# Per-token factors spread over the partitions: transposes of a column read with step zero in place of a diagonal and a product of ones

## The chip, the cores and the metric

The kernel runs on one core of one Trainium2 chip. The metric is the device time of one execution in microseconds (us). The kernel before was run three times: median 2529.21 us, from 2528.57 to 2531.68.

## The reference

Two layers of an encoder over 272 tokens (16 learned meta tokens ahead of 256), model width 2048, all in float32. Per layer:

```
h = rmsnorm(x)                                   # per token: x * rsqrt(mean(x*x) + eps) * g
q, k, v, f, ga, gf = split(h @ w_in)             # 8 query heads, 2 key heads of 128
q, k = rope(rmsnorm(q)), rope(rmsnorm(k))        # per head and token
a = attention(q, k, v) @ w_attn_br
s = real(fft2(f over tokens and group channels)) @ w_four
x = x + (sigmoid(ga + b) * a + sigmoid(gf + b) * s) @ w_out
h2 = rmsnorm(x)
x = x + (silu(conv3(h2 @ w_up_gate)) * (h2 @ w_up_val)) @ w_down
```

The meta tokens are dropped at the end. What matters here is the per-token factor of the norms: one number for each of 272 tokens, four times in the run (two norms in each of two layers), and for the keys one number for each token and each of two key heads, in each layer.

## The kernel before

**Layout.** The residual stream `XT` lies transposed: 128 channels on the partitions, 16 channel tiles, the 272 tokens along the free axis. A factor per token must therefore stand in all 128 partitions as a row of 272 numbers, `rstdB`, before the vector engine can multiply by it.

**Weights.** Each matrix comes in chunks of 512 KB (`raw`, L240, issued from SyncE's queue, four or more ahead). ScalarE rounds a chunk to a high part `wh` (L277), VectorE subtracts for the low part `wl` (L279), and TensorE makes three matmuls per tile, high by high, high by low and low by high (L348 to L350, L416 to L418 in the first groups). `wh` and `wl` have three buffers each, so ScalarE can start on a chunk only when TensorE has left the one three back.

**Order of work.** `group` walks through the chunks. After every second tile of a chunk, that is after six matmuls, it calls `step()` (L290), which lets one of the pending side jobs run one piece. The side jobs are generators pushed with `push`: the norm statistics, the key statistics, the Fourier stages, attention and others. The number that a generator yields is the count of steps that it then waits. `until` and `drain` run steps without matmuls between them. So a job's yields decide between which matmuls its own TensorE instructions stand. The tile framework's planner may still shift instructions against each other on an engine where it is not told to keep the order. Each engine serves its own queue in order.

**Norm statistics** (`norm_stats`, L574). The squares of all channel tiles are added up in `acc`. Three transposes (L582; the 16 meta tokens are repeated to 128 columns in `am`, L576) put the tokens on the partitions, VectorE reduces and scales them to `ms` (L584, L585), and GpSimd raises to the power -0.5 (`pow_half`, L489). `tok` then holds the factors as three columns: column 0 the 16 meta tokens (repeated), columns 1 and 2 the two blocks of 128 tokens. Four steps later VectorE multiplies a constant mask, two identity matrices beside a block for the meta tokens, with the columns of `tok`, which gives the diagonals `dg` (L592, three instructions). Two steps after that one float32 product of a matrix of ones and `dg` sums over the partitions (L595), so that each partition of `ps_nb` holds the whole row. ScalarE copies it to `rstdB` (L596).

**Key statistics** (`kstats`, L943). The same for the keys: transposes in `sums_t` (L911), reduction, power (`rk`), and for each of the two heads a diagonal `dk` (L955, three instructions) and, five steps later, a product with the ones (L958). VectorE multiplies the result into the keys `kp` (L959). Then the keys are swapped by four DMAs from SyncE's queue (L917) and rotated (L921 to L926).

The mask sits in the constants `cst`; mask and identity are loaded together (L426) after the first matmuls. `ones` is set by GpSimd at the start (L468).

Of the kernel before, what the change touches and what calls it, by code (L numbers as in the profile page):

```python
# [10 lines left out]
F32 = mybir.dt.float32  # L11
F32R = mybir.dt.float32r
AF = mybir.ActivationFunctionType
ALU = mybir.AluOpType
AX = mybir.AxisListType

P = 128
D = 2048
NM = 16
SEQ = 256  # L20
T = NM + SEQ
# [52 lines left out]
TH = T // 2 + 2  # L74
BLK = ((0, 16), (16, 144), (144, 272))

C_COS, C_SIN, C_MASK = 0, T, 2 * T
C_ID = 3 * T
C_CC = C_ID + P
C_SC = C_CC + HC1  # L80
C_BR = C_SC + HC1
# [13 lines left out]
def _constants():  # L95
    f32 = np.float32
    pairs = HD // 4
    inv = (f32(1.0) / np.power(f32(ROPE_THETA), np.arange(pairs, dtype=f32) / f32(pairs)).astype(f32)).astype(f32)
    tok = np.arange(SEQ)
    zm = np.zeros(NM, f32)  # L100
    pos_r = np.concatenate([zm, (tok // GRID_W).astype(f32)])
    pos_c = np.concatenate([zm, (tok % GRID_W).astype(f32)])
    ar = (pos_r[None, :] * inv[:, None]).astype(f32).astype(np.float64)
    ac = (pos_c[None, :] * inv[:, None]).astype(f32).astype(np.float64)
    cos = np.concatenate([np.cos(ar), np.cos(ar), np.cos(ac), np.cos(ac)], 0)
    sin = np.concatenate([-np.sin(ar), np.sin(ar), -np.sin(ac), np.sin(ac)], 0)
    eye = np.eye(P)
    m16 = (np.arange(P)[:, None] % NM == np.arange(NM)[None, :]) / (P // NM)
    mask = np.concatenate([m16, eye, eye], 1)
    j = np.arange(P)  # L110
    ang = 2.0 * np.pi * ((j[:, None] * j[None, :]) % P) / P
    cc = (np.cos(ang) / math.sqrt(P))[:, :HC1]
    sc = (np.sin(ang) / math.sqrt(P))[:, :HC1]
    sc[:, 0] = sc[:, HC] = 0.0
    n = np.arange(T)
    angl = 2.0 * np.pi * ((n[:, None] * n[None, :]) % T) / T
    cl = np.cos(angl) / math.sqrt(T)
    sl = -np.sin(angl) / math.sqrt(T)
    b0 = cl[0:128, :TH]
    b1 = sl[1:129, :TH]  # L120
    br = np.zeros((NM, 2, TH))
    br[0:9, 0] = cl[128:137, :TH]
    br[9:16, 1] = sl[129:136, :TH]
    br = np.tile(br.reshape(NM, 2 * TH), (NG, 1))
    gm = (np.arange(P)[:, None] // NM == np.arange(NG)[None, :]).astype(np.float64)
    consts = np.concatenate([cos, sin, mask, eye, cc, sc, br, gm], 1).astype(f32)
    bmat = np.concatenate([b0, b1], 1).astype(f32)
    return np.ascontiguousarray(consts), np.ascontiguousarray(bmat)

# [25 lines left out]
def encoder_kernel(ctx, tc, xT, params, consts, bmat, cfold, csign, w_fl, w_f64c, w_in, w_abr, w_four, w_f64, w_out, w_up, w_down, w_vn, w_dn, w_dt, out):  # L155
# [236 lines left out]
    def first_groups(pss):  # L392
# [4 lines left out]
        for kt in range(KT // CW * 2 * CW):  # L397
# [25 lines left out]
                pump(len(chunks))  # L423
            if kt == 0:
                tc.keep_in_program_order(nc.sync.dma_start(XT[:, 12:16, :], xT[:, 12:16, :]))
                tc.keep_in_program_order(nc.sync.dma_start(cst[:, C_MASK:C_CC], consts[:, C_MASK:C_CC]))  # L426
            step()


# [3 lines left out]
    xH, xL = xHL[:, :, 0, :], xHL[:, :, 1, :]  # L433
    prm = per.tile([P, P_N], F32, name="prm")
    cst = per.tile([P, C_N], F32, name="cst")
    ones = per.tile([P, P], F32, name="ones")
    warm = per.tile([P, 1], F32, name="warm")
    mhalf = per.tile([P, 24], F32, name="mhalf")
    BH = per.tile([P, 2, TH], F32R, name="BH")
# [25 lines left out]
    load_raw(3)  # L465
    st["raw"] = 4
    tc.keep_in_program_order(nc.sync.dma_start(XT[:, 8:12, :], xT[:, 8:12, :]))
    nc.gpsimd.memset(ones, 1.0)  # L468
    nc.gpsimd.memset(V3.bitcast(F32), 0.0)
    nc.gpsimd.memset(o64.bitcast(F32), 0.0)  # L470
    nc.gpsimd.memset(o64m, 0.0)
# [2 lines left out]

    cos = cst[:, C_COS:C_COS + T]
    sin = cst[:, C_SIN:C_SIN + T]
    mask = cst[:, C_MASK:C_MASK + T]
    ident = cst[:, C_ID:C_ID + P]
    ccm = cst[:, C_CC:C_CC + HC1]
    scm = cst[:, C_SC:C_SC + HC1]  # L480
# [68 lines left out]
    def weight_sums():  # L549
# [7 lines left out]
        for s_ in range(1, len(VSETS)):  # L557
# [6 lines left out]
            for q, base, more in kinds:  # L564
                for j in range(NV // 2 + 1):
# [3 lines left out]
                    if j:  # L569
                        issue(dst(q, j - 1), more(j - 1), accum_op=ALU.add, max_dma_last_dim=4096)  # L570
                        ready_sums.update((s_, q, 2 * j - 2 + k) for k in range(2))
                        yield 1

    def norm_stats(holder, gap=0):  # L574
        am = small.tile([P, P // NM, NM], F32, tag="am", name="am", bufs=1)
        nc.vector.tensor_copy(am, _rep(acc[:, 0:NM], P // NM))  # L576
# [9 lines left out]
        tok = small.tile([P, 3], F32, tag="tok", name="tok")  # L586
        pow_half(tok, ms)
        holder["tok"] = tok
        yield 4
        dg = small.tile([P, T], F32, tag="sq", name="dg", bufs=2)  # L590
        for i, (a, b) in enumerate(BLK):
            nc.vector.tensor_scalar(dg[:, a:b], mask[:, a:b], tok[:, i:i + 1], None, op0=ALU.mult)  # L592
        yield 2
        pb = psum.tile([P, 512], F32, tag="aux", name="ps_nb")
        nc.tensor.matmul(pb[:, :T], ones, dg, start=True, stop=True)  # L595
        nc.scalar.copy(rstdB, pb[:, :T])  # L596
        tok2 = small.tile([P, 3], F32, tag="tok2", name="tok2")
        nc.vector.tensor_tensor(tok2, tok, tok, op=ALU.mult)
# [5 lines left out]
    for l in range(DEPTH):  # L604
# [6 lines left out]
        with tc.tile_pool(name=f"mix{l}", bufs=1) as mp:  # L611
# [23 lines left out]
            def ut(name):  # L635
                return mp.tile([P, T], F32, tag="u", name=name, bufs=2)
# [80 lines left out]
            if l == 0:  # L717
# [10 lines left out]
                pss = []  # L728
                push(sums(pss), 4)
                first_groups(pss)  # L730
                for dst, src in ((cst[:, 0:C_MASK], consts[:, 0:C_MASK]), (cst[:, C_CC:], consts[:, C_CC:]), (prm[:, P_BG:], params[:, P_BG:])):
                    tc.keep_in_program_order(nc.sync.dma_start(dst, src))
                bt = rt("bt")
                bt = bt[:, :, :TH]
# [208 lines left out]
            def kstats():  # L943
# [4 lines left out]
                nc.vector.tensor_scalar(kss, kss, 1.0 / HD, EPS, op0=ALU.mult, op1=ALU.add)  # L948
                rk = small.tile([P, 2, 3], F32, tag="rk", name="rk")
                pow_half(rk.rearrange("p a b -> p (a b)"), kss.rearrange("p a b -> p (a b)"))  # L950
                yield 6
                for kv in range(NKV):
                    dk = ut("dk")
                    for i, (a, b) in enumerate(BLK):
                        nc.vector.tensor_scalar(dk[:, a:b], mask[:, a:b], rk[:, kv, i:i + 1], None, op0=ALU.mult)  # L955
                    yield 5
                    pk = psum.tile([P, 512], F32, tag="aux", name="ps_kb")
                    nc.tensor.matmul(pk[:, :T], ones, dk, start=True, stop=True)  # L958
                    nc.vector.tensor_tensor(kp[:, kv, :], kp[:, kv, :], pk[:, :T], op=ALU.mult)  # L959
                yield 3  # L960
                qs = swap(kp)
# [602 lines left out]
```

## Time and profile before

| what | value |
|---|---|
| median of three runs | 2529.21 us |
| the profiled execution | 2531.8 us |
| its span, first to last instruction | 2529.8 us |
| instructions in the span | 47935 |
| mean granted TensorE clock | 1.000 |
| mean DMA rate | 279 GB/s |

The profile is of one execution. The span is a little shorter than the time of that execution, since something lies around it. The engines are PE (TensorE's matmuls), PEld (its weight loads, which overlap the matmuls), DVE (VectorE), ACT (ScalarE), POOL (GpSimd) and SP (SyncE, which issues most DMAs). A group of the profile is named by its line, engine, operation and tiles, `out<-in`; `L592` is line 592 of the kernel before. Matmuls are pipelined and their ends are modelled, so the distance from one start to the next tells what one of them costs, and its own duration does not.

### The profile page before, as it was taken

The numbers are of one execution on the slowest core, as the hardware profiler recorded it, in microseconds if no ns is written. First come the engines' busy times: TensorE is split into PE (matmuls) and PEld (weight loads), VectorE is DVE, ScalarE is ACT, GpSimd is POOL, SyncE is SP. The second block draws the span as 40 slices with busy tenths as digits, with TensorE's granted clock in tenths as the row PEclk, the third lists the DMA queues.
The fourth block names the chain that finished last, engine by engine and source line by source line (L and its number), as shares of the span: only waits on it lengthen the run. The fifth ranks groups of instructions, "written<-read, shape, count | busy, mean of one in ns | idle before, by whom it ended". The sixth has DMA issues, their size and how long they took to land.

```text
span 2529.8 us, 47935 instructions
## 1 busy us (share of the span) xinstructions
PE 2517.8 (100%) x18848; PEld 2435.4 (96%) x18848; DVE 1985.4 (78%) x3151; ACT 1343.6 (53%) x1921; POOL 205.2 (8%) x393
## 2 busy tenths in 40 slices
PE   9999999999999999999999999999999999999999
PEld 9999999999999999999999999999988889998887
DVE  7687866778878667888768887666778787898898
ACT  5455434554444334444445555444676665666665
POOL 0000000012212222222200000000000000000000
PEclk9999999999999999999999999999999999999999
DMA  6444557879999999999975647888888887788887
GB/s 238 164 151 161 192 189 248 260 267 374 393 330 373 398 378 378 386 376 390 384 274 184 201 149 237 258 256 260 272 257 292 297 290 239 258 281 290 276 303 269
DMA packets 194771, 706.85 MB, mean 279 GB/s; under 512 B 22113, under 2 KB 27361, under 8 KB 194289
## 3 DMA queue, kind: packets, MB, share of 16 engines
q1 hardware_dynamic: 146768, 517.09, 58.3%
q0 software_dynamic: 46336, 184.57, 21.1%
q8 instruction: 147, 2.41, 0.4%
q10 hardware_dynamic: 1440, 2.13, 0.2%
q14 instruction: 80, 0.65, 0.1%
HBM read 623.32 MB, written 111.15 MB: 290 GB/s over the span
## 4 chain that ended last, share of the span: by engine, by line
PE 97%; DMA 1%; DVE 1%; ACT 0%; issue 0%; SPq 0%; DVEq 0%; ACTq 0%
PE ps_p L1404 14%; PE ps_ug L350 7%; PE ps_ug L349 7%; PE ps_ug L348 7%; PE ps_d L349 4%; PE ps_uv L349 4%; PE ps_d L348 3%; PE ps_uv L350 3%; PE ps_d L350 3%; PE ps_uv L348 3%; PE ps_o L349 2%; PE ps_o L348 2%; PE ps_o L350 2%; PE ps_gf L349 2%; PE ps_gf L348 2%; PE ps_gf L350 2%
## 5 line engine op out<-in xcount | busy, mean ns | idle before, releaser
L279 DVE TENSOR_TENSOR wl<-raw,wh 128x1024 fp32r<-128x1024 f32 (+1 forms) x961 | 1158.4, 1217 | 408.9 <-ACT wh L277 398.8
L277 ACT CAST wh<-raw 128x1024 fp32r<-128x1024 f32 (+1 forms) x961 | 999.7, 1045 | 900.8 <-PE ps_ug L349 217.2
L349 PE MATMUL ps_ug<-xHL,wh 128*128 128x272 f32 (+1 forms) x1408 | 401.5, 285 | 0.0
L348 PE MATMUL ps_ug<-xHL,wh 128*128 128x272 f32 (+1 forms) x1408 | 400.8, 285 | 0.0
L350 PE MATMUL ps_ug<-xHL,wl 128*128 128x272 f32 (+1 forms) x1408 | 400.4, 286 | 0.0
L349 PEld LDWEIGHTS ps_ug<-xHL,wh 128*128 128x128 f32 x1408 | 264.7, 188 | 3.2
L348 PEld LDWEIGHTS ps_ug<-xHL,wh 128*128 128x128 f32 x1408 | 264.6, 188 | 3.3
L350 PEld LDWEIGHTS ps_ug<-xHL,wl 128*128 128x128 f32 x1408 | 264.0, 188 | 1.4 <-DVE wl L279 1.0
L1404 PE MATMUL ps_p<-wh,opnd 128*128 128x512 f32 x816 | 222.8, 393 | 0.0
L349 PE MATMUL ps_uv<-xHL,wh 128*128 128x272 f32 x704 | 203.3, 289 | 0.0
L349 PE MATMUL ps_d<-gHL,wh 128*128 128x272 f32 x704 | 202.9, 288 | 0.0
L348 PE MATMUL ps_d<-gHL,wh 128*128 128x272 f32 x704 | 202.9, 288 | 0.0
L350 PE MATMUL ps_uv<-xHL,wl 128*128 128x272 f32 x704 | 202.6, 288 | 0.0
L348 PE MATMUL ps_uv<-xHL,wh 128*128 128x272 f32 x704 | 202.3, 287 | 0.0
L350 PE MATMUL ps_d<-gHL,wl 128*128 128x272 f32 x704 | 202.1, 287 | 0.0
L1404 PEld LDWEIGHTS ps_p<-wh,opnd 128*128 128x128 f32 x816 | 148.4, 188 | 29.6 <-ACT wh L277 0.2
L348 PE MATMUL ps_ga<-xHL,wh 128*128 128x272 f32 (+1 forms) x512 | 147.8, 289 | 0.0
L348 PE MATMUL ps_gf<-xHL,wh 128*128 128x272 f32 (+1 forms) x512 | 146.8, 287 | 0.4 <-DVE so L1197 0.4
L510 DVE TENSOR_TENSOR wi<-wi,wi 128x512 f32<-128x512 f32 x224 | 146.9, 684 | 0.0
L349 PE MATMUL ps_o<-mL,wh 128*128 128x272 f32 (+1 forms) x512 | 146.5, 286 | 0.0
L349 PE MATMUL ps_ga<-xHL,wh 128*128 128x272 f32 (+1 forms) x512 | 146.1, 285 | 0.0
L350 PE MATMUL ps_o<-mH,wl 128*128 128x272 f32 (+1 forms) x512 | 146.1, 285 | 0.0
(378 smaller groups left out, 5970.2 us busy)
## 6 DMA issues: line engine op xcount, KB each, us to landing
raw<-in_w_up SPq DMA_DIRECT2D x288, 512.0 KB, 6.4
raw<-in_w_in SPq DMA_DIRECT2D x191, 512.0 KB, 3.9
raw<-in_w_down SPq DMA_DIRECT2D x88, 512.0 KB, 6.9
wi<-in_w_dn POOLq DMA_DIRECT2D x80, 512.0 KB, 8.9
ft<-wi POOLq DMA_DIRECT2D x80, 512.0 KB, 7.4
raw<-ft SPq DMA_DIRECT2D x80, 512.0 KB, 4.6
raw<-in_w_out SPq DMA_DIRECT2D x64, 512.0 KB, 4.3
raw<-fv SPq DMA_DIRECT2D x64, 512.0 KB, 4.8
```

What stands on the lines that cost most here:

```text
L277: nc.scalar.copy(h[:, a:b], r[:, a:b])
L279: nc.vector.tensor_tensor(lo[:, a:b], r[:, a:b], h[:, a:b].bitcast(F32), op=ALU.subtract)
L348: nc.tensor.matmul(o, h[:, c, sl], a, start=kt == 0, stop=False)
L349: nc.tensor.matmul(o, h[:, c, sl], b, start=False, stop=False)
L350: nc.tensor.matmul(o, lo[:, c, sl], a, start=False, stop=kt == nk - 1)
L510: tt = lambda *v, **kw: tc.keep_in_program_order(nc.vector.tensor_tensor(*v, **kw))
L1404: nc.tensor.matmul(ps[h], x, w[:, 512 * h:512 * h + 512], start=fresh and (s_, q) in BEGIN and first, stop=(s_, q) in END and end, skip_gr ...
```

## The change

A helper `spread` takes a column of factors and, for each of the three token blocks, makes a transpose on TensorE: the column is read with step zero along the free axis, so that it looks like a block of 128 equal columns; its transpose has the factors along the free axis, the same in all 128 partitions. `spread` takes the place of diagonal and product in `norm_stats` and in `kstats`. The two yields around the diagonal become one: in `norm_stats` 4 and 2 become 5; in `kstats` 6, and 5 for each head, become 7 for both heads together. The meta tokens' block takes 16 partitions and a 16 by 16 identity. The mask leaves the constants (272 columns fewer in `cst` and in the load at L426), and `ones` goes with its memset.

```diff
@@ -74,8 +74,8 @@
 TH = T // 2 + 2
 BLK = ((0, 16), (16, 144), (144, 272))
 
-C_COS, C_SIN, C_MASK = 0, T, 2 * T
-C_ID = 3 * T
+C_COS, C_SIN = 0, T
+C_ID = 2 * T
 C_CC = C_ID + P
 C_SC = C_CC + HC1
 C_BR = C_SC + HC1
@@ -105,8 +105,6 @@
     cos = np.concatenate([np.cos(ar), np.cos(ar), np.cos(ac), np.cos(ac)], 0)
     sin = np.concatenate([-np.sin(ar), np.sin(ar), -np.sin(ac), np.sin(ac)], 0)
     eye = np.eye(P)
-    m16 = (np.arange(P)[:, None] % NM == np.arange(NM)[None, :]) / (P // NM)
-    mask = np.concatenate([m16, eye, eye], 1)
     j = np.arange(P)
     ang = 2.0 * np.pi * ((j[:, None] * j[None, :]) % P) / P
     cc = (np.cos(ang) / math.sqrt(P))[:, :HC1]
@@ -123,7 +121,7 @@
     br[9:16, 1] = sl[129:136, :TH]
     br = np.tile(br.reshape(NM, 2 * TH), (NG, 1))
     gm = (np.arange(P)[:, None] // NM == np.arange(NG)[None, :]).astype(np.float64)
-    consts = np.concatenate([cos, sin, mask, eye, cc, sc, br, gm], 1).astype(f32)
+    consts = np.concatenate([cos, sin, eye, cc, sc, br, gm], 1).astype(f32)
     bmat = np.concatenate([b0, b1], 1).astype(f32)
     return np.ascontiguousarray(consts), np.ascontiguousarray(bmat)
 
@@ -423,7 +421,7 @@
                 pump(len(chunks))
             if kt == 0:
                 tc.keep_in_program_order(nc.sync.dma_start(XT[:, 12:16, :], xT[:, 12:16, :]))
-                tc.keep_in_program_order(nc.sync.dma_start(cst[:, C_MASK:C_CC], consts[:, C_MASK:C_CC]))
+                tc.keep_in_program_order(nc.sync.dma_start(cst[:, C_ID:C_CC], consts[:, C_ID:C_CC]))
             step()
 
 
@@ -433,7 +431,6 @@
     xH, xL = xHL[:, :, 0, :], xHL[:, :, 1, :]
     prm = per.tile([P, P_N], F32, name="prm")
     cst = per.tile([P, C_N], F32, name="cst")
-    ones = per.tile([P, P], F32, name="ones")
     warm = per.tile([P, 1], F32, name="warm")
     mhalf = per.tile([P, 24], F32, name="mhalf")
     BH = per.tile([P, 2, TH], F32R, name="BH")
@@ -465,7 +462,6 @@
     load_raw(3)
     st["raw"] = 4
     tc.keep_in_program_order(nc.sync.dma_start(XT[:, 8:12, :], xT[:, 8:12, :]))
-    nc.gpsimd.memset(ones, 1.0)
     nc.gpsimd.memset(V3.bitcast(F32), 0.0)
     nc.gpsimd.memset(o64.bitcast(F32), 0.0)
     nc.gpsimd.memset(o64m, 0.0)
@@ -474,7 +470,6 @@
 
     cos = cst[:, C_COS:C_COS + T]
     sin = cst[:, C_SIN:C_SIN + T]
-    mask = cst[:, C_MASK:C_MASK + T]
     ident = cst[:, C_ID:C_ID + P]
     ccm = cst[:, C_CC:C_CC + HC1]
     scm = cst[:, C_SC:C_SC + HC1]
@@ -571,6 +566,11 @@
                         ready_sums.update((s_, q, 2 * j - 2 + k) for k in range(2))
                         yield 1
 
+    def spread(ps, cols):
+        for i, (a, b) in enumerate(BLK):
+            n = b - a
+            nc.tensor.transpose(ps[:, a:b], cols[0:n, i:i + 1].to_broadcast([n, P]), ident[0:n, 0:n])
+
     def norm_stats(holder, gap=0):
         am = small.tile([P, P // NM, NM], F32, tag="am", name="am", bufs=1)
         nc.vector.tensor_copy(am, _rep(acc[:, 0:NM], P // NM))
@@ -586,13 +586,9 @@
         tok = small.tile([P, 3], F32, tag="tok", name="tok")
         pow_half(tok, ms)
         holder["tok"] = tok
-        yield 4
-        dg = small.tile([P, T], F32, tag="sq", name="dg", bufs=2)
-        for i, (a, b) in enumerate(BLK):
-            nc.vector.tensor_scalar(dg[:, a:b], mask[:, a:b], tok[:, i:i + 1], None, op0=ALU.mult)
-        yield 2
+        yield 5
         pb = psum.tile([P, 512], F32, tag="aux", name="ps_nb")
-        nc.tensor.matmul(pb[:, :T], ones, dg, start=True, stop=True)
+        spread(pb, tok)
         nc.scalar.copy(rstdB, pb[:, :T])
         tok2 = small.tile([P, 3], F32, tag="tok2", name="tok2")
         nc.vector.tensor_tensor(tok2, tok, tok, op=ALU.mult)
@@ -728,7 +724,7 @@
                 pss = []
                 push(sums(pss), 4)
                 first_groups(pss)
-                for dst, src in ((cst[:, 0:C_MASK], consts[:, 0:C_MASK]), (cst[:, C_CC:], consts[:, C_CC:]), (prm[:, P_BG:], params[:, P_BG:])):
+                for dst, src in ((cst[:, 0:C_ID], consts[:, 0:C_ID]), (cst[:, C_CC:], consts[:, C_CC:]), (prm[:, P_BG:], params[:, P_BG:])):
                     tc.keep_in_program_order(nc.sync.dma_start(dst, src))
                 bt = rt("bt")
                 bt = bt[:, :, :TH]
@@ -948,14 +944,10 @@
                 nc.vector.tensor_scalar(kss, kss, 1.0 / HD, EPS, op0=ALU.mult, op1=ALU.add)
                 rk = small.tile([P, 2, 3], F32, tag="rk", name="rk")
                 pow_half(rk.rearrange("p a b -> p (a b)"), kss.rearrange("p a b -> p (a b)"))
-                yield 6
+                yield 7
                 for kv in range(NKV):
-                    dk = ut("dk")
-                    for i, (a, b) in enumerate(BLK):
-                        nc.vector.tensor_scalar(dk[:, a:b], mask[:, a:b], rk[:, kv, i:i + 1], None, op0=ALU.mult)
-                    yield 5
                     pk = psum.tile([P, 512], F32, tag="aux", name="ps_kb")
-                    nc.tensor.matmul(pk[:, :T], ones, dk, start=True, stop=True)
+                    spread(pk, rk[:, kv])
                     nc.vector.tensor_tensor(kp[:, kv, :], kp[:, kv, :], pk[:, :T], op=ALU.mult)
                 yield 3
                 qs = swap(kp)
```

## The prediction

> **What bounds the kernel now.** I read the page's engine totals first, then the page's shares of the chain of work that ended last, then the view of waits for TensorE alone (who waits on whom: us in total, times, longest).
>
> ```profile
> PE 2517.8 (100%) x18848; PEld 2435.4 (96%) x18848; DVE 1985.4 (78%) x3151; ACT 1343.6 (53%) x1921; POOL 205.2 (8%) x393
> PE 97%; DMA 1%; DVE 1%; ACT 0%; issue 0%; SPq 0%; DVEq 0%; ACTq 0%
> ```
>
> ```profile
> PE ps_f L416 <- ACT wh L277: 5.4, 2, 4.5
> PE ps_s L384 <- DVE wl L279: 0.9, 1, 0.9
> PE ps_s L383 <- ACT wh L277: 0.8, 1, 0.8
> PE ps_uv L345 <- DVE wl L279: 0.7, 2, 0.4
> PE ps_gf L348 <- DVE so L1197: 0.4, 1, 0.4
> PE ps_fa L667 <- DVE E L646: 0.2, 1, 0.2
> ```
>
> The first line: TensorE (PE) shows work for 2517.8 of 2529.8 us. A busy PE in this profile need not be at its peak, so the second line is the better witness: 97% of the chain that set the end lies on PE. The other six lines are every wait of PE above the view's threshold. 5.4 us belong to the first loads; the remaining five groups sum to 0.9 + 0.8 + 0.7 + 0.4 + 0.2 = 3.0 us. So an edit can gain in two ways only: fewer PE instructions, or a share of those 3.0 us. It can lose by any new wait in PE's queue, which is served in order.
>
> **What the old and the new way cost PE.** Durations of matmuls overlap, so the price of one is the step that the starts take. The chain in order of time gives it merged (start, us, what):
>
> ```profile
> 81.79 0.66 PE ps_ss L911 x6
> 91.62 0.92 PE ps_kb L958 x4
> 108.25 0.44 PE ps_ss L911 x4
> 543.59 0.46 PE ps_nb L595 x2
> ```
>
> The product of ones and the diagonal (L595, L958) is float32 and leaves two records, which take 0.46 us together. The two calls of three 128x128 float32 transposes each (L911) leave six records, one per transpose, and take 0.66 / 6 = 0.11 us apiece; the four at 108.25 give the same. The groups of the tiles give the counts (after the colon: shortest, median and longest in ns, first and last start):
>
> ```profile
> L595 PE MATMUL ps_nb<-dg,ones x8: 391/392/393, 41.2 to 1834.2; 128*128 128x272 f32 x8
> L958 PE MATMUL ps_kb<-dk,ones x8: 390/392/393, 91.5 to 1356.7; 128*128 128x272 f32 x8
> L592 DVE TENSOR_SCALAR dg<-cst,tok x12: 233/280/396, 39.5 to 1831.9; 128x128 f32<-128x128 f32 x8, 128x16 f32<-128x16 f32 x4
> L955 DVE TENSOR_SCALAR dk<-cst,rk x12: 224/278/279, 85.5 to 1350.8; 128x128 f32<-128x128 f32 x8, 128x16 f32<-128x16 f32 x4
> ```
>
> Removed: 8 products (four norms, two layers times two key heads), 8 x 0.46 = 3.7 us of PE. Added: 8 x 3 transposes, of 16, 128 and 128 columns. The two of 128 columns I price as the rows: 0.11 each. Two things about them no row shows.
>
> The first is the transpose of only 16 columns. If its price went with the columns it would be 0.11 x 16 / 128 = 0.01 us. The nearest row with few columns is the float32 product of L667 and L668, 65 columns, two records each:
>
> ```profile
> 48.58 0.39 PE L667 MATMUL ps_fa<-cst,E 128*128 128x65 f32 x2
> 48.80 0.39 PE L668 MATMUL ps_fa<-cst,E 128*128 128x65 f32 x2
> ```
>
> From 48.58 to 48.80 a pair takes 0.22 us, 0.11 per record, though by columns it should take 0.46 x 65 / 272 = 0.11 for the pair. So float32 records here have a floor near 0.11 us, whatever their columns, and I take 0.11 for the 16-column transpose too; the lower end, 0.01, stays in the range and would gain 8 x 0.10 = 0.8 us more.
> [...]
>
> The second is the step of zero. The column is the stationary operand: each of n partitions is read 128 times at one address while the weights are loaded. No PE row reads so. The lower bound is no extra cost, 0.11 us per transpose. For the upper bound the farthest row is the float32 product itself, with two records of 0.23 us each: if the broadcast transpose needed a pair like that, it would cost 0.46 us instead of 0.11. I take no extra cost: DVE reads a repeated 16-column block in the same manner for `am` (L576), 128 elements in 0.23 us, where a plain copy of 272 takes 0.30 (L501), so repeating an address is not dear there; and this is the row that it is nearest to in kind.
>
> ```profile
> 4.32 0.30 DVE L501 COPY acc<-sq 128x272 f32<-128x272 f32 x1
> 30.61 0.23 DVE L576 COPY am<-acc 128x128 f32<-128x128 f32 x1
> ```
>
> **PE sum:** 24 x 0.11 = 2.6 us added, 3.7 removed: **-1.0 us**, all on the path.
>
> **Vector, scalar, GpSimd and DMA.** 24 vector instructions of about 0.28 us go, some 6 us of DVE. DVE is 78% busy and behind PE: the view of waits shows the scalar engine held up for a free weight buffer until PE is done with it, and DVE then held up by the scalar engine.
>
> ```profile
> DVE wl L279 <- ACT wh L277: 412.6, 438, 5.0
> ACT wh L277 <- PE ps_ug L349: 217.2, 119, 2.4
> ```
>
> So the 6 us fall into DVE's idle time and are worth nothing, save a share of the 3.0 us above. The densest stretch that they leave is this one (columns: length, then busy PE, PEld, DVE, ACT, POOL with counts, clock, DMA share, GB/s):
>
> ```profile
> 1340.00:1360.00 20.00, 20.00 (x161) 19.84 (x160) 18.72 (x43) 10.22 (x18) 1.70 (x3) 1.00 0.45 158
> 1600.00:1610.00 10.00, 8.71 (x71) 8.38 (x70) 9.77 (x22) 5.85 (x11) 0.70 (x2) 1.00 0.76 267
> ```
>
> DVE has 18.72 of 20 us there, and still PE lost nothing. Where PE does lose, 1600 to 1610, no removed instruction is near (the last `dk` starts at 1350.8). The memset of `ones` goes from POOL's idle start: nothing. The constants of L426 shrink by 272 of 400 columns, 136 of its 200 KB, and go out at 12.7 us. From 13.4 us PE takes a matmul every 0.13 us and waits for nothing, so this too is covered.
>
> ```profile
> 12.72 0.42 SPq L426 DMA_DIRECT2D cst<-in_consts  x1
> 13.39 0.29 PE L416 MATMUL ps_f<-xHL,wh 128*128 128x272 f32 x1
> 13.52 0.29 PE L417 MATMUL ps_f<-xHL,wh 128*128 128x272 f32 x1
> ```
>
> **The moved wait.** Before, DVE waited for the factor from POOL (L489) and PE came later, for the finished diagonal. Now PE itself waits for POOL, and it comes earlier: in the compiled order the norm transposes stand 6 matmuls (6 x 0.13 = 0.8 us) ahead of the old product, the key transposes of both heads 24 matmuls (3.1 us) ahead of the first old one. Behind a waiting transpose stands every later matmul. POOL's rows against PE's:
>
> ```profile
> 37.69 1.80 POOL L489 TENSOR_TENSOR tok<-ms,mhalf 128x3 f32<-128x3 f32 x1 [33.94 <-DVE ms L585]
> 84.12 1.33 POOL L489 TENSOR_TENSOR rk<-kss,mhalf 128x6 f32<-128x6 f32 x1 [14.40 <-DVE kss L948]
> 541.18 0.88 POOL L489 TENSOR_TENSOR tok<-ms,mhalf 128x3 f32<-128x3 f32 x1 [10.34 <-DMA raw<-in_w_up]
> 1336.30 0.88 POOL L489 TENSOR_TENSOR tok<-ms,mhalf 128x3 f32<-128x3 f32 x1 [7.31 <-DVE ms L585]
> 1346.97 1.45 POOL L489 TENSOR_TENSOR rk<-kss,mhalf 128x6 f32<-128x6 f32 x1 [9.79 <-DVE kss L948]
> 1830.64 0.88 POOL L489 TENSOR_TENSOR tok<-ms,mhalf 128x3 f32<-128x3 f32 x1 [15.46 <-DVE ms L585]
> ```
>
> ```profile
> 41.15 0.62 PE L595 MATMUL ps_nb<-dg,ones 128*128 128x272 f32 x2
> 91.46 1.08 PE L958 MATMUL ps_kb<-dk,ones 128*128 128x272 f32 x4
> 543.43 0.62 PE L595 MATMUL ps_nb<-dg,ones 128*128 128x272 f32 x2
> 1338.47 0.62 PE L595 MATMUL ps_nb<-dg,ones 128*128 128x272 f32 x2
> 1352.38 0.62 PE L958 MATMUL ps_kb<-dk,ones 128*128 128x272 f32 x2
> 1834.02 0.62 PE L595 MATMUL ps_nb<-dg,ones 128*128 128x272 f32 x2
> ```
>
> POOL's result is ready (its start plus its length), and PE arrives (its old start less the lead), at: 39.5 and 40.4; 85.5 and 88.3; 542.1 and 542.7; 1337.2 and 1337.7; 1348.4 and 1349.3; 1831.5 and 1833.2. The slack is 0.9, 2.9, 0.6, 0.5, 0.9 and 1.7 us: thin, but positive everywhere, and DVE's instructions before POOL's power are the same or fewer. I cost the wait at nothing; without that cover it is the lateness of POOL, six times.
>
> What the transposes free earlier (`rstdB`, the keys, one step or more) feeds DVE and ACT work that PE does not wait for. In layer 1 the planner deals the fold's and keys' DVE work out anew around 1340 to 1390; with DVE off the path I price that at nothing, with a swing of 1 us either way.
>
> **Sum.** The profiled execution took 2531.8 us, its span 2529.8 and 2.0 around it: 2531.8 - 1.0 = 2530.8. That execution lies 2.6 us above the median of the three runs, 2529.21, so for the median: 2529.2 - 1.0 = **2528.2 us**, 0.04% less. About 0.2%, 5.1 us, is what a measurement of this kernel can tell from no change.
>
> **Rivals.**
> - *The step of zero makes the weight load slow* (slower). Place: 24 transposes in PE's queue. At 0.46 us each they cost 11.0 us, less 3.7: 2529.2 + 7.3 = 2536.5. It undoes the gain from 0.15 us per transpose (3.7 / 24) and passes 0.2% from (3.7 + 5.1) / 24 = 0.37. For it: no PE row reads such an operand. Against it: the DVE row. Chance 6% for over 0.2%, 8% for a milder form, 2529 to 2533. [...]
> - *PE waits for POOL.* If the semaphore or POOL is later than shown, by the first call's 1.80 against 0.88 us, that is 0.9 us at the three norms with the short call; the slacks 0.6, 0.5 and 1.7 leave 0.3 + 0.4 + 0. So +0.7: 2528.9. Chance 8%.
> - *The stalls of the later stages shrink* because DVE is freer and the order is dealt anew: up to the 3.0 us above, 2528.2 - 3.0 = 2525.2; a fall of over 5.1 us would need start or end as well. Chance 10% for a good part of it, of which 4% beyond 0.2%.
> - *The change does not do what it says*: the transposes also leave two records of 0.11, 24 x 0.22 = 5.3, less 3.7: +1.6, 2530.8. Against it: the six transposes of L911 left six records. Chance 4%.
>
> **How the numbers follow.** The forecast has the remaining 64%. Runs of the same program spread over 3.1 us (2528.57 to 2531.68), so a median of a few moves by about 1 us. The range 2525.2 to 2531.2 holds the forecast, POOL's wait, the doubled records and most of the shrinking stalls, with part of the milder slow load; the strong slow load and a fall beyond 0.2% stay out. Faster by over 0.2%: 4%, rounded up to 5%. Slower: 6%, with 1% for what I did not name: 7%. Within: 88%.
>
> **What would show it.** Right: the two float32 products gone, 24 records with 0.11 us to the next start, PE without a wait at L572 on POOL, PE's other waits within 1 us of 8.4 in sum, 24 DVE instructions fewer. Wrong: a step of 0.2 us or more between the broadcast transposes; an idle PE put down to `tok` or `rk`; new waits on `wl` between 1340 and 1610.

## The result, and the profile after

The kernel after took 2540.01 us (median of six runs, 2537.56 to 2542.32) beside 2529.41 us of the kernel before (six runs, 2528.57 to 2531.68): ratio 1.0038, 95% interval 1.0028 to 1.0048. It is **slower by 10.6 us** (0.4%), beyond the range and on the other side of the forecast. The profiled execution took 2540.18 us with a span of 2538.4 us.

The engine totals of the kernel after:

```profile
PE 2525.2 (99%) x18856; PEld 2442.2 (96%) x18856; DVE 1981.9 (78%) x3127; ACT 1343.7 (53%) x1921; POOL 204.9 (8%) x392
```

PE has 8 records more (16 of the products gone, 24 come) and 7.4 us more busy time; DVE has 24 instructions fewer. Next, the waits of PE of 0.3 us and more in the kernel after:

```profile
PE ps_f L414 <- ACT wh L275: 5.4, 3, 4.5
PE ps_f L837 <- DVE wl L277: 1.7, 1, 1.7
PE ps_q L348 <- DVE wl L277: 1.4, 1, 1.4
PE ps_uv L343 <- DVE wl L277: 0.3, 1, 0.3
PE ps_uv L342 <- ACT wh L275: 0.3, 1, 0.3
```

No wait on `tok` or `rk`, but two that are new, both on `wl`, 3.1 us together. The windows view gives their place, and a second thing that the waits don't show. First the kernel before, then the kernel after (columns as in the prediction; the clock is the figure behind POOL's count):

```profile
600.00:700.00 100.00, 100.00 (x801) 100.00 (x800) 85.28 (x164) 45.03 (x58) 21.40 (x40) 1.00 1.00 385
900.00:950.00 50.00, 50.00 (x400) 50.00 (x399) 33.68 (x43) 17.89 (x17) 10.18 (x19) 1.00 1.00 381
1385.00:1388.00 3.00, 2.96 (x26) 2.73 (x25) 2.96 (x6) 2.36 (x5) 0.00 (x0) 1.00 0.59 191
```

```profile
600.00:700.00 100.00, 100.00 (x797) 100.00 (x796) 85.12 (x162) 44.39 (x57) 21.41 (x40) 1.00 0.99 382
900.00:950.00 50.00, 50.00 (x401) 50.00 (x400) 33.14 (x40) 17.35 (x17) 10.72 (x20) 1.00 1.00 385
1385.00:1388.00 3.00, 1.32 (x11) 1.10 (x10) 2.27 (x4) 0.65 (x1) 0.00 (x0) 1.00 0.00 0
1388.00:1392.00 4.00, 4.00 (x23) 3.92 (x23) 3.15 (x4) 1.99 (x2) 0.00 (x0) 0.57 0.73 224
1600.00:1610.00 10.00, 10.00 (x86) 10.00 (x85) 6.39 (x10) 5.14 (x9) 0.71 (x2) 1.00 0.91 295
```

Four readings. From 600 to 700, in the up-projection of layer 0, PE is busy all the time in both kernels at full clock, waits for nothing, and still gets through 797 matmuls instead of 801: each takes 0.5% longer. From 900 to 950, in the down-projection, the count is the same (400, 401). From 1385 to 1388 PE stands for 1.7 us, and over the four microseconds behind that the granted clock is 0.57 on average. From 1600 to 1610 the stall of before (8.71 us busy there) is gone.

For the whole run I took the same matmuls in two traces and subtracted their starts. Columns: the place in the kernel before, in us; entries: how much later the matmul starts, in us, each from one profiled execution. The kernels below the first line are the experiments.

| kernel | 405 | 1205 | 1345 | 1410 | 1560 | 1610 | 2520 |
|---|---|---|---|---|---|---|---|
| after | 0.7 | 3.1 | 3.3 | 8.4 | 9.0 | 6.6 | 8.4 |
| e9: after, old waits | 2.1 | 4.5 | 4.6 | 4.9 | 5.4 | 3.8 | 5.2 |
| e1: after, old places | -0.4 | -0.4 | -0.4 | 6.0 | 6.0 | 4.4 | 4.8 |
| e4: all spreads, old places and waits | -0.4 | -0.5 | -0.5 | -0.4 | -0.3 | -2.5 | -2.8 |
| e2: before, weights 64 bytes off | 0.2 | 2.3 | 2.4 | 2.5 | 3.1 | 0.8 | 3.5 |
| e10: new key waits alone | -1.2 | -1.4 | -1.4 | 3.4 | 3.5 | 1.9 | 1.9 |

In the kernel after there is a slow creep up to 1345 and a jump of 5.1 us between 1345 and 1410; 2.4 us come back before 1610. In every kernel of the table 1.6 to 2.4 us come back there, in e2 too, which has the instructions of before.

**What changed besides the instructions.** The compiled programs show two things that the diff doesn't say. *Places:* mask (1088 bytes per partition) and `ones` (512) stood in memory ahead of the buffers `raw`, `wh`, `wl` and most others. Without them all these lie 1600 bytes lower, while `xHL`, which lies ahead of them, stays at a multiple of 128. 1600 is 64 modulo 128: `xHL` lay 96 bytes from `wh`, counted modulo 128 (place of `xHL` less that of `wh`), and now lies 32 from it. *Order:* with the new waits of the keys, VectorE's compiled order in layer 1 has the fold's work (L770 to L784), the keys' rotation and the low parts of V in one heap, with few `wl` between.

The theories. **Theory one: two causes that add**, the distance of `xHL` and weights modulo 128 bytes, and the order of layer 1; beside them a spread that costs a little more than the product. Rivals: one of the two causes alone makes it all; or a tile's own place counts and not the distance; or the step of zero.

### The profile page after: what moved, and what is told of

The parts are those of the page before. It is cut to its first block, busy times and chain, and to the rows that moved or that the text cites. A ratio compares the mean times of both kernels' runs of the same rounds, so it can differ in the third digit from the quotient of the medians.

```text
span 2538.4 us, 47916 instructions
## 1 busy us (share of the span) xinstructions
PE 2525.2 (99%) x18856; PEld 2442.2 (96%) x18856; DVE 1981.9 (78%) x3127; ACT 1343.7 (53%) x1921; POOL 204.9 (8%) x392
## 3 DMA queue, kind: packets, MB, share of 16 engines
q10 hardware_dynamic: 1440, 2.13, 0.2%
## 5 line engine op out<-in xcount | busy, mean ns | idle before, releaser
L346 PE MATMUL ps_gf<-xHL,wh 128*128 128x272 f32 (+1 forms) x512 | 147.5, 288 | 0.1
L347 PE MATMUL ps_gf<-xHL,wh 128*128 128x272 f32 (+1 forms) x512 | 146.2, 286 | 0.0
```

Of the source, the lines that this page charges most:

```text
L346: nc.tensor.matmul(o, h[:, c, sl], a, start=kt == 0, stop=False)
L347: nc.tensor.matmul(o, h[:, c, sl], b, start=False, stop=False)
```

## The experiments

A difference is against the runs of the kernel before on the same chip. Of e5 to e8, e14 and e15 there is one run each, so only 3 us or more mean something in their times; their traces are read for the counts.

**e1: the kernel after with the old places.** 400 columns more behind `warm` put all that follows back.

```diff
-    warm = per.tile([P, 1], F32, name="warm")
+    warm = per.tile([P, 401], F32, name="warm")[:, 0:1]
```

> The changed kernel with 1600 bytes of unused space in each partition behind the constants, so that weights and activations lie again where they lay before (only some tiles of the mixing stage stay 1024 bytes lower). Three theories. Placement: the change moved the weight buffers by 1600 bytes against xHL, and that made every matmul of the xHL stages about 0.5 ns slower (797 instead of 801 matmuls in 600 to 700 us); then the count returns to 801 and the time falls by 4 to 5 us, to about 2535. Order: the key factors that are all due at once let the planner pile up the vector work of layer 1 between 1355 and 1390 us, which stalls TensorE for about 3 us and drops its clock; then this stays, and the rest over the 2529.4 of before, about 5 us, is it. Rival, the transposes alone: nothing changes, 2540 and 797.

Measured: 2536.54 us beside 2529.89, ratio 1.0021 [1.0011, 1.0032]. Its waits, then a window:

```profile
PE ps_f L837 <- DVE wl L277: 1.5, 1, 1.5
PE ps_q L348 <- DVE wl L277: 1.4, 1, 1.4
```

```profile
600.00:700.00 100.00, 100.00 (x800) 100.00 (x800) 85.03 (x162) 44.63 (x58) 21.33 (x40) 1.00 1.00 383
```

The count is back (800) and with it the creep is gone, the stall stays: the places are one cause and not the only one.

**e2, e7, e8, e12: the kernel before, everything behind `ones` moved** by 64, 32, 128 and 96 bytes (16, 8, 32 and 24 columns). The distance, 96 before, becomes 32, 64, 96 and 0.

```diff
-    ones = per.tile([P, P], F32, name="ones")
+    ones = per.tile([P, P + 16], F32, name="ones")[:, :P]
```

> The kernel before with 64 unused bytes behind the tile of ones: no instruction and no order changes, every later tile moves by 64 bytes (1600 is 64 over a multiple of 128 and of 512). Placement with a period of 128 bytes: 797 matmuls in 600 to 700 us instead of 801 and 4 to 5 us more, about 2534. If places do not matter, or only in another way than the offset within 128 bytes: 801 and 2529.4. Order and the transposes alone expect 2529.4 too.

> The kernel before with everything behind ones moved by 32 bytes. Theory one: xHL stands 96 bytes (modulo 128) from the weights before, 32 with the change, 64 here, which is the offset of gHL in the down projection's stage; so 799 in 600 to 700 us, between the two. A theory of a period of 64 bytes is dead already, since 64 changed the step. If only alignment to 64 counts, this may be far worse or far better than either.

> The kernel before with everything behind ones moved by 128 bytes. A period of 128 bytes: 801 matmuls in 600 to 700 us and the time of before, 2529 to 2532. A longer period (the change moved by 1600, which is 64 over a multiple of 512): some other count, 797 or between.

> The kernel before with 96 bytes more behind the ones, so that the offset of xHL to the weights is 0 modulo 128 bytes (measured so far: 96 gives 800 to 801 matmuls in 600 to 700 us and 2529 to 2530 us, 64 gives 798 and 2535.6, 32 gives 797 and 2535.8). Theory one names no value for 0. If the cost falls with the distance from 32, 0 is like 64: 798 and about 2535.5. If the cost comes from reading both in one place of the 128 bytes, 0 is the worst: below 797 and above 2537. If 96 is no optimum, 0 could be better: above 801 and below 2528.

Measured: e2 (distance 32) 2535.79 beside 2529.89, ratio 1.0024 [1.0015, 1.0033]; e7 (64) 2535.56 and e8 (96 again) 2529.31 beside 2530.39; e12 (0) 2530.49 beside 2529.32, ratio 1.0004 [0.9995, 1.0012]. One window of each, in the order of distances 32, 64, 96 and 0:

```profile
600.00:700.00 100.00, 100.00 (x797) 100.00 (x797) 85.27 (x163) 44.80 (x58) 21.32 (x40) 1.00 0.99 379
```

```profile
600.00:700.00 100.00, 99.85 (x798) 99.64 (x797) 84.38 (x161) 45.08 (x58) 21.33 (x40) 1.00 0.99 378
```

```profile
600.00:700.00 100.00, 100.00 (x800) 100.00 (x799) 85.04 (x163) 44.87 (x58) 21.33 (x40) 1.00 1.00 378
```

```profile
600.00:700.00 100.00, 100.00 (x800) 100.00 (x800) 84.86 (x163) 45.27 (x58) 21.34 (x40) 1.00 0.99 383
```

No instruction differs from the kernel before, nor does the order on any engine, and 64 unused bytes cost 5.9 us. 128 bytes cost nothing (e8, one run), so a period of 128 fits. In the whole time distance 0 can't be told from 96; neither guess that I gave for it as a loss was met.

A count of matmuls takes in waits as well. The pace itself is the mean time from one start to the next of the up-projection's matmuls (`ps_ug`, steps of 0.19 us and more left out), in ns; layer 0 has 272 columns, layer 1 only 258:

| distance | kernels | layer 0 | layer 1 |
|---|---|---|---|
| 96 | before, e6, e8 | 125.27, 125.27, 125.38 | 119.52, 119.51, 119.33 |
| 32 | after, e9, e2, e5 | 125.85, 125.85, 125.72, 125.71 | 120.43, 120.45, 120.78, 120.45 |
| 64 | e7 | 125.36 | 120.91 |
| 0 | e12 | 125.35 | 120.27 |

So in layer 0 only the distance of 32 is slow. The 798 of e7 are no slower pace: its window shows PE busy for 99.85 of 100 us, and two of its steps at 652 take 0.43 and 0.23 us. In layer 1 the distances 64 and 0 are slow too, and most of e7's loss lies there.

The trace of e8 shows one thing more, from 1600 to 1610:

```profile
1600.00:1610.00 10.00, 10.00 (x85) 9.95 (x85) 9.40 (x20) 6.06 (x12) 0.52 (x1) 1.00 0.90 319
```

The stall that the profile of before has here (8.71 us busy) is gone, with before's instructions in before's order.

**e5, e6, e15: which tiles.** e5 puts 64 bytes ahead of `wh` and 64 behind `wl`; e15 puts 64 between `wh` and `wl`, so that `wl` and what follows move and `wh` does not; e6 moves `xHL` too:

```diff
-    XT = per.tile([P, KT, T], F32, name="XT")
+    XT = per.tile([P, KT * T + 16], F32, name="XT")[:, :KT * T].rearrange("p (k t) -> p k t", k=KT)
```

> The kernel before, in which only the buffers wh and wl move by 64 bytes (two unused gaps of 64 bytes, one ahead of wh and one behind wl, so that all behind moves by 128 and raw and xHL not at all). Theory one, the offset between the moving operand and the weights counts, with a period of 128 bytes: 797 matmuls in 600 to 700 us instead of 801, and the down projection's stage, 880 to 980 us, where gHL moved by 128 and the weights by 64, changes as well from its 799 or 800. Theory two, the places of what the vector and scalar engines and the DMAs touch count: 801 and 799, as in before. Theory three, the weights' own place counts: 797, and 799 in the second stage, as there was with all moved by 64.

> The kernel before with 64 unused bytes behind XT: xHL and everything behind it move by 64 bytes together, only XT stays. Theory one (offset between moving operand and weights): 801 matmuls in 600 to 700 us, as before. Theories two and three (own place of the other engines' tiles, or of the weights): 797.

> The kernel before with 64 bytes between the high and the low weights: the low ones, and what lies behind, are moved by 64, the high ones stay. Two of three matmuls read the high weights. Theory one, if each matmul pays for its own weights' offset to xHL: a third of the loss of 4 in 801, so 799 to 800 matmuls in 600 to 700 us, and about 2531 us. Rival (only the high weights matter): 801, 2529. Rival (the low ones alone matter, or the two may not differ): 797 or 798, 2535.

Measured: e5 2538.02 and e6 2531.03 beside 2530.39, e15 2531.93 beside 2530.61. e5 gets through 798 matmuls from 600 to 700. From 900 to 950 it gets through 401, so the down-projection, whose own distance changed by 64, did not change as theory one expected. By e7's expectation that distance went from 64 to 0, which the table finds alike for 272 columns. The window of e6 and that of e15:

```profile
600.00:700.00 100.00, 100.00 (x800) 100.00 (x799) 85.06 (x162) 44.38 (x58) 21.33 (x40) 1.00 1.00 385
```

```profile
600.00:700.00 100.00, 100.00 (x801) 100.00 (x800) 84.27 (x163) 45.39 (x58) 21.32 (x40) 1.00 0.99 380
```

In e6 the weights lie in the very place that they have in e2, but `xHL` is moved with them: 800, and in its trace no creep. So it is the distance and not a place. In e15 the high weights have the old distance and the low ones 32: 801. Moving the low weights alone makes no loss, so the loss needs the high ones; the high ones alone at 32 were not run. By the subtracted starts, e5 loses another 4.9 us and e2 2.1 us behind 2000 us. In e2 the up-projection of layer 1 accounts for that (2.3 us, see the table); in e5 4.3 us lie in the matmuls of `ps_p` (128x512), and why is left open.

**e3, e4: the spreads at the old places.** In both, mask and `ones` stay where they were. e3 has the diff's norms alone (with its `yield 5`); e4 has all spreads, but the waits of before: 6 steps in the norms, 6 and then 5 for each head in the keys. Beside the kernel after, e4's waits differ so:

```diff
-        yield 5
+        yield 6
...
-                yield 7
+                yield 6
                 for kv in range(NKV):
+                    yield 5
                     pk = psum.tile([P, 512], F32, tag="aux", name="ps_kb")
                     spread(pk, rk[:, kv])
```

> Only the four norms are spread by transposes (yield 5); keys, mask, ones and every tile's place stay as before. After's trace has a spread of three at 0.52 us against 0.46 for the product, so four of them cost 0.2 us more. Order and placement: no new stall, 801 matmuls in 600 to 700 us, about 2529.6. Transposes alone as cause of the 10.6 us: half of it, about 2534 or more.

> All eight spreads by transposes, but with the old yields (norms 6 steps, keys 6 and then 5 for each head) and with mask and ones still in place, so that nearly all tiles lie where they lay. Order and placement: the loss goes, 8 x 0.06 = 0.5 us over before, about 2530. Transposes alone: about 2540. If placement is right and order wrong: 2534 to 2535, with the stall of layer 1 still there.

Measured beside 2529.89: e3 2530.88, ratio 1.0005 [0.9996, 1.0014]; e4 2529.04, ratio 0.9998 [0.9989, 1.0006]. Of e4:

```profile
600.00:700.00 100.00, 100.00 (x801) 100.00 (x800) 85.33 (x162) 44.54 (x58) 21.31 (x40) 1.00 1.00 382
1380.00:1400.00 20.00, 19.95 (x172) 19.47 (x171) 18.47 (x27) 13.24 (x19) 0.00 (x0) 1.00 0.77 246
```

With places and waits kept, eight spreads instead of eight products can't be told from the kernel before.

**e9: the places alone.** The kernel after with the waits of e4, by the diff just shown; nothing else.

> The kernel after with its lower places (weights 1600 bytes lower, offset of xHL to the weights 32 modulo 128 bytes), but with the waits of before: 6 steps in the norms, 6 and then 5 for each head in the keys. Theory one (two causes that add, the places and the order): only the places are left, so about 2535.5 us (2534.5 to 2537), 797 matmuls in 600 to 700 us, no wait of PE on wl between 1360 and 1400. Rival (the lower places also bring about the stall in layer 1): about 2540, with that wait.

Measured: 2536.85 beside 2529.32, ratio 1.0026 [1.0017, 1.0035]. Its window:

```profile
600.00:700.00 100.00, 100.00 (x797) 100.00 (x797) 85.29 (x164) 45.27 (x60) 20.28 (x38) 1.00 0.99 383
```

The stall of layer 1 is gone (its longest wait on `wl` is 0.6 us, near 304), the 797 are there.

**e10: the order alone.** The kernel before with the spreads in the keys only, and the diff's `yield 7`; all places kept.

> The kernel before, all places kept, with the spreads in the keys alone and the new wait of 7 steps for both heads. Theory one (the order that follows from the 7 steps is a cause of its own): waits of PE on wl at 1370 and 1386, about +6 between 1340 and 1410, some 1.6 back near 1600: 2534 to 2536.5 us, 800 or 801 matmuls in 600 to 700 us. Rival (the stall needs the other norm, or other places): 2530, no such wait.

Measured: 2534.59 beside 2529.32, ratio 1.0021 [1.0011, 1.0030]. One execution of 10646 us, far out of line with every other, is left out of the ratio. Its waits, then a window:

```profile
PE ps_f L846 <- DVE wl L279: 1.5, 1, 1.5
PE ps_q L350 <- DVE wl L279: 1.4, 1, 1.4
```

```profile
600.00:700.00 100.00, 100.00 (x800) 100.00 (x799) 84.67 (x162) 44.62 (x57) 20.97 (x40) 1.00 0.99 380
```

The stall is there, at full pace (800).

How it comes about is read from VectorE in time order. In the kernel before, the query's rotation at 1375 found its swapped halves ready after 0.22 us:

```profile
1375.04 0.72 DVE L921 TENSOR_TENSOR qs<-qs,cst 128x544 f32<-128x544 f32 x1 [0.22 <-DMA qs<-qp]
```

In the kernel after:

```profile
1361.52 1.23 DVE L277 TENSOR_TENSOR wl<-raw,wh 128x1024 fp32r<-128x1024 f32 x1
...
1370.60 2.36 DVE L277 TENSOR_TENSOR wl<-raw,wh 128x1024 fp32r<-128x1024 f32 x2
...
1382.84 0.73 DVE L917 TENSOR_TENSOR qs<-qs,cst 128x544 f32<-128x544 f32 x1 [2.98 <-DMA qs<-qp]
...
1386.37 1.22 DVE L277 TENSOR_TENSOR wl<-raw,wh 128x1024 fp32r<-128x1024 f32 x1
```

Between the first two `wl` stand 16 other lines and 9 us: PE's first wait, 1.4 us up to 1371.88. SyncE's queue shows what that does to the swap of the query. Before, then after (start, time that the issues took):

```profile
1371.06 2.52 SPq L917 DMA_DIRECT2D qs<-qp  x4
```

```profile
1371.89 4.33 SPq L238 DMA_DIRECT2D raw<-fw  x3
1376.38 2.52 SPq L913 DMA_DIRECT2D qs<-qp  x4
```

The four DMAs go out 5.3 us later, of which the creep up to here makes 3.3, right behind three weight loads, and land by 1382.84. VectorE idles 2.98 us for them with the `wl` of 1386.37 queued behind (ScalarE had its `wh` done at 1381.52): PE's second wait, 1.7 us up to 1387.64. That the 7 steps bring this order about is shown by e10 against e4 and e9. The trace of e10 has the same chain at the old places: the four DMAs go out at 1371.67 behind three weight loads, VectorE idles 2.13 us for them, and the `wl` of 1381.42 ends PE's wait at 1382.69. No run breaks a single link of the chain; it is read from these two traces.

**e11: no step of zero.** Old places and waits, but one VectorE copy writes each column out 128 times, and the transposes read that.

```diff
+    def widen(cols):
+        nc.vector.tensor_copy(big, cols.unsqueeze(2).to_broadcast([P, 3, P]))
...
-            nc.tensor.transpose(ps[:, a:b], cols[0:n, i:i + 1].to_broadcast([n, P]), ident[0:n, 0:n])
+            nc.tensor.transpose(ps[:, a:b], big[0:n, i, :], ident[0:n, 0:n])
```

> Old places, old waits, spreads everywhere, but VectorE first writes each column out 128 times (one copy with 128 x 3 x 128 elements), and the transposes read that with step one. Theory (the step of zero is what takes 0.16 us per transpose, a plain one takes 0.11): three transposes stand 0.05 us apart less, a norm's spread takes 0.33 us of PE instead of 0.52, so 8 x 0.46 less 24 x 0.11, about 1 us below the kernel before and 1.5 below the kernel with step zero, old places and old waits: 0.9995 of before. Rival (the 0.16 us belong to this place in the queue, not to the step of zero): the starts stay 0.16 us apart and the time within 0.5 us of before.

Measured: 2530.49 beside 2529.32, ratio 1.0004 [0.9995, 1.0012]. The spread of the second norm in PE's time order, first in the kernel after, then in e11:

```profile
543.34 0.29 PE L348 MATMUL ps_ug<-xHL,wl 128*128 128x272 f32 x1
543.56 0.59 PE L572 MATMUL ps_nb<-cst,tok 16*128 16x16 f32 x3
543.90 0.37 PE L346 MATMUL ps_ug<-xHL,wh 128*128 128x272 f32 x1
544.11 0.29 PE L347 MATMUL ps_ug<-xHL,wh 128*128 128x272 f32 x1
```

```profile
543.41 0.29 PE L348 MATMUL ps_ug<-xHL,wl 128*128 128x272 f32 x1
543.63 0.60 PE L576 MATMUL ps_nb<-cst,big 16*128 16x16 f32 x3
543.98 0.37 PE L346 MATMUL ps_ug<-xHL,wh 128*128 128x272 f32 x1
544.19 0.28 PE L347 MATMUL ps_ug<-xHL,wh 128*128 128x272 f32 x1
```

From the matmul ahead to the second one behind: 544.11 - 543.34 = 0.77 us, and 544.19 - 543.41 = 0.78. The rival has it: the step of zero costs nothing that can be told here, and my explanation fell.

**e13, e14: the block of 16 rows.** Both are the kernel after with the old waits and 64 bytes more behind `cst`, so that the weights lie 1536 = 12 x 128 bytes lower and the distance is 96. In e13 the meta tokens' block, too, is a transpose over all 128 partitions; in e14 the 16-row block comes last.

```diff
         for i, (a, b) in enumerate(BLK):
-            n = b - a
-            nc.tensor.transpose(ps[:, a:b], cols[0:n, i:i + 1].to_broadcast([n, P]), ident[0:n, 0:n])
+            nc.tensor.transpose(ps[:, a:a + P], cols[:, i:i + 1].to_broadcast([P, P]), ident)
```

> The kernel after with the waits of before, 64 bytes more behind cst so that the weights lie 1536 = 12 x 128 bytes lower and the offset to xHL is 96 again, and with all three transposes over 128 partitions: the meta tokens' block too reads all rows of its column and the whole identity (its 112 surplus columns are written over by the next transpose). Since plain transposes of written-out columns stood 0.16 us apart as well, the step of zero is not what costs. Theory (the 16-row block is what costs: it makes TensorE finish one shape before the next): the starts are 0.11 us apart, from the matmul before to the second after some 0.58 us instead of 0.77, 8 x 0.19 = 1.5 us below the kernel with all spreads, old places and old waits (0.9998 of before): 0.9992 of before, about 2527.5. Rival (the place of the output, columns 16 and 144 of its bank, or what stands ahead in the queue): the starts stay 0.155 to 0.16 apart, 2529. Places: 800 or 801 matmuls in 600 to 700 us; if the period of 128 bytes doesn't hold, 797 and 2535.

> As before, but with the 16-row transpose kept at 16 rows and put last of the three. Theory (a change of shape costs, where it stands): the two of 128 rows are 0.11 us apart, about 0.2 us stand around the small one, the whole stays near 0.77 us from the matmul before to the second after. Rival (the output's columns cost): the two large ones stay 0.155 to 0.16 us apart.

Measured: e13 2530.79 beside 2530.61, ratio 1.0002 [0.9993, 1.0011]; e14 2533.65. PE in time order, e13 and e14, then two of e13's waits and one of its windows:

```profile
545.31 0.29 PE L348 MATMUL ps_ug<-xHL,wl 128*128 128x272 f32 x1
545.43 0.49 PE L571 MATMUL ps_nb<-cst,tok 128*128 128x128 f32 x3
545.68 0.37 PE L346 MATMUL ps_ug<-xHL,wh 128*128 128x272 f32 x1
545.89 0.28 PE L347 MATMUL ps_ug<-xHL,wh 128*128 128x272 f32 x1
```

```profile
544.18 0.29 PE L348 MATMUL ps_ug<-xHL,wl 128*128 128x272 f32 x1
544.31 0.54 PE L572 MATMUL ps_nb<-cst,tok 128*128 128x128 f32 x3
544.77 0.39 PE L346 MATMUL ps_ug<-xHL,wh 128*128 128x272 f32 x1
545.01 0.29 PE L347 MATMUL ps_ug<-xHL,wh 128*128 128x272 f32 x1
```

```profile
PE ps_fa L662 <- DVE E L641: 1.5, 1, 1.5
PE ps_f L836 <- DVE wl L277: 1.0, 1, 1.0
```

```profile
50.00:54.00 4.00, 4.00 (x24) 4.00 (x24) 3.05 (x15) 1.08 (x6) 0.00 (x0) 0.67 0.03 5
```

e13: 545.89 - 545.31 = 0.58 us, as foretold for one shape; by the raw starts the three stand 0.109 us apart. e14: 545.01 - 544.18 = 0.83: the two large ones stand 0.109 apart and the small one pays behind them, more than I expected (0.77). So the block of 16 rows among 128 is the price. The whole of e13 is not the 1.5 us better: other waits came, a late `E` in the first 60 us, behind which the clock falls as well (0.67), and a `wl` in layer 1.

**e16, e17: one shape, old places.** e4 with e13's transposes; in e17 the keys wait 5 steps and then 5 per head.

> All places and waits of before, mask and ones kept in their places, all spreads with transposes over 128 partitions. Its compiled vector order in the first 60 us is that of the kernel with 16-row blocks at the same places and waits, without the late E of the kernel with all rows and lower places; in layer 1 it is that of the latter (kernel all rows: 1.0 us of waiting on wl near 1386). By the sum: 8 x 0.46 less 24 x 0.11, 1.0 us less than before on the path, the 1.0 of waiting back: 0.9995 to 1.0002 of before. Rival (the transposes' gain of 1 us can be told in the whole time): below 0.9992.

> The same with 5 steps ahead of the keys' spreads in place of 6 (then 5 for each head, as before). The compiled vector order in layer 1 puts the keys' work at the place that it has in the kernel with 16-row blocks and no stall. If order alone makes the 1.0 us on wl near 1386, it goes: 0.9990 to 0.9998 of before, the best of all. Rival: it stays, like the one before.

Measured beside 2529.74: e16 2530.05, ratio 0.9998 [0.9989, 1.0007]; e17 2528.18, ratio 0.9993 [0.9984, 1.0002]. e17 has no wait on `wl` there, e16 has its 1.0, at 1379. e17's median is the lowest of all, but its interval holds 1: no version is shown to beat the kernel before.

## Why the prediction was wrong

**The sum of -1.0 us** failed at the 16-column transpose, "I take 0.11 for the 16-column transpose too". The spread takes 0.77 us from the matmul ahead to the second behind, less two plain steps of 0.125: 0.52 us, against 0.46 for the product by the same rule. Eight times +0.06 is +0.5 us instead of -1.0. The floor of 0.11 held for records of one shape (e13: three in 0.33); the change of shape was priced nowhere. The prediction took the nearest row by its columns (L667). The kernel before has a row that is near by its rows: L865, a float32 product over 16 rows between two over 128, all with 130 columns.

```profile
1415.36 0.38 PE L864 MATMUL ps_fa<-cf,E 128*128 128x130 f32 x2
1415.68 0.48 PE L865 MATMUL ps_fa<-sg,e 16*128 16x130 f32 x2
1416.09 0.49 PE L866 MATMUL ps_fa<-cf,E 128*128 128x130 f32 x2
```

By the raw starts the step inside the first pair is 0.110 us; into the 16-row pair, inside it and out of it the steps are 0.204, 0.215 and 0.200. So a price near 0.2 us stood in the trace at hand, and since the columns are equal it goes with the rows or their change.

e13 against the kernel after, 0.58 against 0.77 us, shows such a price for the transposes too. Why TensorE takes longer there is not shown.

**The step of zero**, the uncertainty to which I gave most of the slow side, costs nothing that can be told (e11: 0.77 beside 0.78 us).

**The planner's new order**, "I price that at nothing, with a swing of 1 us either way", is the first large miss. The two waits are 3.1 us. Then the clock: in the trace it is granted at half for 3.41 us from 1388 on, which costs about half of that, 1.7. Together 4.8 of the jump of 5.1. The premise, "with DVE off the path", failed: VectorE is no busier than before (78% of the span in both kernels, and from 1340 to 1360 14.49 of 20 us beside 18.72), but what counts is in which order its queue holds `wl` and a wait for a DMA (2.98 us for the swap, ahead of the `wl` of 1386.37). The listed sign, new waits on `wl` between 1340 and 1610, was the right one to watch.

**The places** are the second, and stand nowhere in the prediction, so they were put at nothing without a reason: I read the end of mask and `ones` as one memset and a shorter load. e9 shows their price with the old waits, 7.5 us (2536.85 - 2529.32).

**Whether the two simply add** can't be told. Against its own runs of before, e4 (neither) stands at -0.85 us, e9 (places) at +7.5, e1 (order) at +6.7, the kernel after at +10.6, 3.6 us less than the two together; but each of these figures has an interval of about 2.5 us either way. The other pair, e2 (+5.9) and e10 (+5.3), comes to 11.2. The table shows where e9 and e1 differ from the kernel after: e9 is 1.4 us later already at 405, and in e1's trace the half clock lasts 6.83 us instead of 3.41, some 1.7 us more. Why either is so is not shown.

**Right** were: PE never waits for POOL at the moved place (no `tok`, no `rk` among the waits); VectorE's 24 instructions, worth nothing by themselves (e4); and, as a number, the rival of the shrinking later stall: 1600 to 1610 gives 2.4 us back. That was luck. The stall goes in e8 as well, where VectorE is no freer and no order is dealt anew, so it needs no edit to go. Some traces have a part of it (e6, e15), others do not (e2, e8, e12). The profiled execution of before lies 2.6 us above the median of its three runs, so it does not tell how much of the 3.0 us of waits was there to gain.

## What to carry to other kernels

Where a change takes a tile away, list which tiles move with it, and compare the compiled order of every engine far beyond the edit; both can cost ten times what the edited instructions do (here 7.5 us in e9 and 5.3 in e10, beside the 0.5 estimated for eight spreads). Before a wait in one profile is counted as something to gain, see whether a second execution has it. Price a new instruction by a row of its own shape, rows as well as columns. An experiment on a change should first put places and waits back, so that what is left is the instruction itself. Keep a run of TensorE instructions in one shape: a block of 16 rows cost more than a full one (0.77 us in the kernel after, 0.58 in e13).

## What the runs showed of the hardware

- The distance modulo 128 bytes between moving operand and high weights changes the pace of back-to-back matmuls. With 272 columns a step takes 125.3 to 125.4 ns at 96, 64 and 0, and 125.7 to 125.9 at 32 (801 and 797 per 100 us); with 258 columns 119.3 to 119.5 at 96, 120.3 at 0, 120.4 to 120.8 at 32 and 120.9 at 64 (before, after, e2, e5 to e9, e12; 64 and 0 from one trace each). The down-projection, whose moving operand `gHL` moved along with the weights in the kernel after, kept its 400 in 50 us. What in the memory does it is not shown.
- Waits of PE of 1.5 to 1.8 us were followed by half the clock for 3.41 us (after 1.7, e10 1.5, e13 1.5, e17 1.8) or 6.83 us (e1, 1.5); waits of 1.4 (after, at 1371.88) and 1.3 us (e4) were not. The length of one wait does not decide it: e17 and e15 have half the clock for 3.41 us from 1602 on too, behind waits of 0.3 and 0.9 us and of 0.6 and 0.9 us, and before has waits of 0.8 and 0.9 us at the same place with none. In the 3.41 us ahead of each of these falls PE was idle for 1.15 to 1.79 us. What sets a fall and its length is not shown.
- In the kernel after, a 16-row transpose between 128-row instructions delays itself (0.216 us behind a matmul instead of 0.125) and each of the two behind it (0.156 and 0.159 instead of the 0.109 of e13). A 16-row product in the kernel before (L865) takes steps of 0.20 to 0.215 us where the pair ahead of it takes one of 0.110.
